# A hybrid decoder block: tile-wise pool waits, later value loads, products two groups behind their rows, and a gate tile taken into attention

## The chip, the cores and the metric

The kernel runs on one core of a Trainium2 chip. The metric is the device time of one execution in microseconds (us). The engines named below are TensorE (PE; its weight loads are PEld), VectorE (DVE), ScalarE (ACT), GpSimd (POOL) and SyncE (SP). Every DMA of this kernel is issued by SP, in one queue.

## The reference, cut to what matters

All is float32; S = D = 1024.

```python
h = rms_norm(x, g_pre)
qa, ka, va, fa, za, qb, kb, vb, zb, gates = split(h @ w_in)
# forgetting attention, 8 heads of 64: logits + c_t - c_s, c = cumsum(log_sigmoid(fa + b_forget))
ya = merge(softmax_causal(qa ka^T / 8 + c_t - c_s) va) * silu(za)
# differential attention, 4 heads: two softmaxes of 64-wide rotated q, k; values 128 wide
yb = (softmax_causal(q1 k1^T / 8) - lam * softmax_causal(q2 k2^T / 8)) vb
yb = merge(rms_norm(yb, g_subln) * (1 - lam_init)) * silu(zb)
gate_a, gate_b = split(sigmoid(gates))
merged = gate_a * (ya @ w_branch[0]) + gate_b * (yb @ w_branch[1])
x = x + rms_norm(merged @ w_out, g_post)
```

## The kernel before, in words

Float32 products are made from rounded high and low parts: a = hi + lo, and hi*hi + hi*lo + lo*hi are three matmuls. Five stages follow each other.

1. Value stage (0 to 111 us). x is normed and transposed to hT (1024 x 1024, in 128 x 512 blocks, high and low), and the values va, vb are projected and spilled to DRAM (va_d, vb_d).
2. Attention (111 to 604 us): units u = 0 to 3 are differential heads, u = 4 to 7 are pairs of forgetting heads. A unit's q and k are projected in 128 x 512 chunks (`project`, L246, 24 matmuls into pq or pk). For differential units `rope` copies the chunk out of PSUM (L283, ScalarE), swaps its halves by four DMAs of 64 KB (L287: swk, swq) and combines both (L288 to L290, VectorE and GpSimd). `stack` (L295 to L298) makes the high and low operands TA, TB, KA, KB; `swapped` (L407) makes by two DMAs the operands X0 and X1 with the partition halves exchanged. A group is two rows of queries: `s_row` multiplies (Sd or Sf, L421, L422), VectorE adds the bias and takes the maximum (L423), ScalarE the exponential (L428), GpSimd the scaling (L542). `av` transposes the rows on TensorE (ptd or ptf, L450), splits them into phf (L453, ScalarE) and plf (L454, VectorE), and multiplies by the values V (L474) into ypd or ypf, a PSUM pool (yps) with one buffer; `evac` empties it (L551 ScalarE, L552 VectorE) and stores it to y_d.
   Between the groups the list `fill` places other work: the next unit's projections, the z projections (pz, spilled to z_d), and the block sums t_d of hT.
3. Gate stage (604 to 750 us). The gate columns for output columns d = 0 (two tiles, one for each branch, of two chunks of 24 matmuls, `gates_plain`) are projected plainly; for d = 1 to 7 a Winograd scheme with seven half-size products is used (`wino`, L713), on the block sums loaded by `h_load` (T, eight loads of 1 MB, L795).
4. Branch stage (750 to 855 us, L846), 5. output stage (to the end).

The code is written in one order; a scheduler of the language then gives each engine its own order by its estimates of when inputs are ready. A pool hands out buffers by tag. Where a pool takes over memory that another pool has given back, its first users wait for the old pool's last users. Each engine runs its instructions in its order.

The lambda loads `lt` (L572) feed a few small VectorE instructions and one exponential (L575 to L581) ahead of the first unit.

The value loads come first in each unit:

```python
            def load():
                nc.sync.dma_start(f32(vt), src)
...
        pend = None
        for u in range(8):
            load, groups = unit_attn(u, T)
...
                for r in rws:
                    r()
                if pend:
                    pend()
                pend = prd
```

Of the kernel before, what the change touches and what calls it, by code (L numbers as in the profile page):

```python
# [16 lines left out]
P = 128  # L17
# [29 lines left out]
def tile_hybrid_block(  # L47
# [201 lines left out]


    with ExitStack() as st:
        qk = st.enter_context(tc.tile_pool(name="qk", bufs=2))
        pp = st.enter_context(tc.tile_pool(name="pp", bufs=6))
        ptp = st.enter_context(tc.tile_pool(name="ptp", bufs=3))
        stg = st.enter_context(tc.tile_pool(name="stg", bufs=2))
        pj = st.enter_context(tc.tile_pool(name="pj", bufs=2, space=PSUM))
        sps = st.enter_context(tc.tile_pool(name="sps", bufs=3, space=PSUM))
        tps = st.enter_context(tc.tile_pool(name="tps2", bufs=2, space=PSUM))
        yps = st.enter_context(tc.tile_pool(name="yps", bufs=1, space=PSUM))

        nc.sync.dma_start(gsub, g_subln.rearrange("o p -> p o"))
        nc.gpsimd.tensor_scalar(gsub, gsub, 1.0 - LAM_INIT, 1.0, op0=ALU.mult, op1=ALU.mult)
# [64 lines left out]
        def z_tasks(t):  # L327
            return spill_tasks(f"z{t}", (ZA + t * P) if t < 4 else (ZB + (t - 4) * P), z_d[t])

        def spill_tasks(nm, c0, dst):  # L330
            box = {}

            def mk(c):
                def run():
                    if not box:
                        box[0] = load_w(nm, w_cols(c0))
                    ps = pj.tile([P, CH], F32, tag="pj", name=f"p{nm}_{c}")
                    project(ps, box[0], c)
                    zs = stg.tile([P, CH], F32, tag="raw", name=f"s{nm}_{c}", bufs=3)
                    nc.scalar.copy(zs, ps)  # L340
                    nc.sync.dma_start(dst[:, c * CH:(c + 1) * CH], zs)
                return run
            return [mk(0), mk(1)]
# [57 lines left out]
        def swapped(T, m, g, nm):  # L401

            src = T["TB" if m else "TA"]
            qs = slice(2 * g * P, (2 * g + 2) * P)
            t = qk.tile([P, 2 * P], F32R, tag=f"X{m}", name=f"X{m}{nm}_{g}", bufs=3)
            for a, b in ((UPR, DNR), (DNR, UPR)):
                nc.sync.dma_start(f32(t[a]), f32(src[b, qs]))  # L407
            return t

        def s_row(T, m, i, X, bias, boff, nm):  # L410

# [73 lines left out]
        def unit_attn(u, T):  # L485

            diff = u < 4
            t = u if diff else u - 4
            vt = qk.tile([P, NB, 256], F32R, tag="V", name=f"V{u}")
            src = (vb_d if diff else va_d)[:, t, :].rearrange("(b p) c -> p b c", p=P)  # L490
            cb = []
            groups = []

            def load():
                nc.sync.dma_start(f32(vt), src)
                if not diff:
                    for m in range(2):
                        b = big.tile([P, S], F32, tag="big", name=f"cb{u}_{m}")
                        h = 2 * t + m
                        nc.sync.dma_start(b, cum_d[h:h + 1, :].to_broadcast([P, S]))  # L500
                        cb.append(b)

            if diff:
                def row(i, rows):
                    boff = S - (i + 1) * P
                    if "X" not in rows:
                        rows["X"] = [swapped(T, m, i // 2, f"d{u}") for m in range(2)]
                    p1, l1 = s_row(T, 0, i, rows["X"][0], dmask, boff, f"d{u}")
                    p2, l2 = s_row(T, 1, i, rows["X"][1], dmask, boff, f"d{u}")
                    n = (i + 1) * P  # L510
                    nc.vector.tensor_tensor(l2, l2, nlam, op=ALU.mult)  # L511
                    nc.gpsimd.tensor_scalar(  # L512
                        p2[:, 0:n], p2[:, 0:n], l2, 1.0, op0=ALU.mult, op1=ALU.mult)
                    nc.scalar.activation(p1[:, 0:n], p1[:, 0:n], AF.Copy, scale=l1)
                    nc.gpsimd.tensor_tensor(
                        p1[:, 0:n], p1[:, 0:n], p2[:, 0:n], op=ALU.add)
                    rows[i] = p1

                def evac(g):
                    def run(yp):  # L520
                        ys = stg.tile([P, 2 * P], F32, tag="ys", name=f"ys{u}_{g}")
                        nc.scalar.copy(ys, yp)
                        nc.sync.dma_start(y_d[u][:, g * 2 * P:(g + 1) * 2 * P], ys)
                    return run

                for g in GORD[u]:
                    rows = {}
                    groups.append((
                        4 * g + 3,
                        [lambda i=i, rows=rows: row(i, rows) for i in (2 * g, 2 * g + 1)],  # L530
                        lambda g=g, rows=rows: av(rows, g, vt, 0, False, evac(g), f"d{u}_{g}", False)))
            else:
                ysb = {}

                def row(m, i, rows):
                    n = (i + 1) * P
                    diag = cb[m][:, n - P:n]
                    nc.gpsimd.tensor_tensor(diag, diag, trim, op=ALU.add)  # L538
                    if "X" not in rows:
                        rows["X"] = swapped(T, m, i // 2, f"f{u}")  # L540
                    p1, l1 = s_row(T, m, i, rows["X"], cb[m], 0, f"f{u}")
                    nc.gpsimd.tensor_scalar(  # L542
                        p1[:, 0:n], p1[:, 0:n], l1, 1.0, op0=ALU.mult, op1=ALU.mult)
                    rows[i] = p1

                def evac(m, g):
                    def run(yp):
                        if m == 0:
                            ysb[g] = stg.tile([P, 2 * P], F32, tag="ys", name=f"ys{u}_{g}")
                        tmp = stg.tile([P, 2 * P], F32, tag="yt", name=f"yt{u}_{m}_{g}", bufs=1)  # L550
                        nc.scalar.copy(tmp[64:128], yp[64:128])  # L551
                        nc.vector.tensor_tensor(  # L552
                            ysb[g][64 * m:64 * m + 64], yp[0:64], tmp[64:128], op=ALU.add)
                        if m == 1:
                            nc.sync.dma_start(y_d[u][:, g * 2 * P:(g + 1) * 2 * P], ysb[g])
                    return run

                for g in GORD[u]:
                    for m in range(2):
                        rows = {}  # L560
                        groups.append((
                            4 * g + 3,
                            [lambda m=m, i=i, rows=rows: row(m, i, rows) for i in (2 * g + 1, 2 * g)],
                            lambda m=m, g=g, rows=rows: av(
                                rows, g, vt, m * P, True, evac(m, g), f"f{u}_{m}_{g}",
                                u == 7 and g in FING)))
            return load, groups


        lt = pp.tile([P, 4, 64], F32, tag="P", name="lt")  # L570
# [43 lines left out]
        T, tasks = unit_proj(0)  # L614
        for tk in tasks:
            tk()
        pend = None
        for u in range(8):
            load, groups = unit_attn(u, T)
            if u == 1:  # L620
                forget_sums()
            load()
# [10 lines left out]
            total = sum(s[0] for s in groups)  # L633
            done, nf = 0, 0
            for n, (wgt, rws, prd) in enumerate(groups):
                for r in rws:
                    r()
                if pend:
                    pend()
                pend = prd  # L640
                done += wgt
                while nf < len(fill) and nf < len(fill) * done / total:
                    fill[nf]()
                    nf += 1
        pend()

    bigs.close()

# [3 lines left out]


    gw = ExitStack()
    wx = gw.enter_context(tc.tile_pool(name="wx", bufs=2))
    tmp = gw.enter_context(tc.tile_pool(name="tmp", bufs=8))
    ydp = gw.enter_context(tc.tile_pool(name="ydp", bufs=1))
    xst = ExitStack()
    xps = xst.enter_context(tc.tile_pool(name="xps", bufs=8, space=PSUM))

    def split(dst, src, eng=nc.vector):

# [82 lines left out]


    tst = ExitStack()
    tpool = tst.enter_context(tc.tile_pool(name="tpool", bufs=1))

    yz = {}  # L750

# [24 lines left out]
        nc.sync.dma_start(g_d[d][br][:, c * CH:(c + 1) * CH], g)  # L776

    def gates_plain(d):
        for br in range(2):
            wt = load_w(f"g{br}_{d}", w_cols(GT + br * D + d * P), True, True)  # L780
            for c in range(2):
                ps = xps.tile([P, CH], F32, tag="x", name=f"pg{d}_{br}_{c}")
# [5 lines left out]
             for m, (kh, sh) in hB.items()}  # L788

    def h_load():  # L790
        for m in (4, 6, 5, 7):
            ts = [tpool.tile([P, 4, CH], F32R, tag=f"T{m}{part}", name=f"T{m}{part}")
                  for part in range(2)]
            for part in range(2):
                nc.sync.dma_start(f32(ts[part]), t_d[m][part])  # L795
            h_ops[m] = [[t[:, k, :] for k in range(4)] for t in ts]

    def gates_pair(d, order):
        raw = []
# [19 lines left out]
    tst.close()  # L819


    mpool = gw.enter_context(tc.tile_pool(name="mpool", bufs=1))
    mg = mpool.tile([P, KT, S], F32, name="mg")
    hslot = {(kh, sh): [(hpool, f"h{part}{kh}{sh}") for part in range(2)]
             for kh in range(2) for sh in range(2)}
# [202 lines left out]
```

## Time and profile before

| | |
|---|---|
| median of 3 runs | 946.88 us (944.96 to 947.32) |
| the profiled execution | 945.37 us |
| its span in the profile | 943.3 us |
| mean granted TensorE clock | 0.988 of full speed |
| busy: PE, DVE, ACT, POOL | 895.5, 625.4, 435.8, 489.3 us |
| DMA over the span | 136.95 MB, mean 145 GB/s |

A time in a profile row is from the start of the span. A row of the order of time has start, duration, engine, line, operation, output<-inputs, shapes and count, and in brackets how long the engine stood idle before it and which instruction ended that wait. A matmul of 512 columns that follows another starts 0.23 us after it, though its row says 0.39, since matmuls overlap.

### The profile page before, as it was taken

Reading aid. Unit: us, or ns where it says so; the run is one execution under the profiler, and the core shown is the slowest. Engines: PE = TensorE matmul, PEld = TensorE weight load, DVE = VectorE, ACT = ScalarE, POOL = GpSimd, SP = SyncE. Lnnn points to the kernel's source line nnn. Section 1 sums busy time; section 2 is a strip of 40 time slices with the busy share of each in tenths; the row PEclk is TensorE's granted clock in tenths of the full one; section 3 lists DMA queues with packets and bytes.
Section 4 is the critical chain, followed back from the end, with each engine's and each line's share of the span. In section 5 each row is a group of like instructions: output and inputs, shape, how many; then the busy total and the mean of one; then the engine's idle time right before and its main releaser. Section 6 shows DMA issues by size and latency. Waiting matters only on the chain. (4 is left out here: it accounts for less than half of the span.)

```text
span 943.3 us, 13785 instructions
## 1 busy us (share of the span) xinstructions
PE 895.5 (95%) x4600; PEld 750.5 (80%) x4600; DVE 625.4 (66%) x1180; ACT 435.8 (46%) x862; POOL 489.3 (52%) x461
## 2 busy tenths in 40 slices
PE   7999989999999999999999998899999999999993
PEld 5899868787887888888878887788888888887872
DVE  6731248988767778577767558515868893559766
ACT  3421115575656766465755648524443450324331
POOL 7200024446546448364554566407667436878963
PEclk9999999999999999999999999999999999999997
DMA  9532354424316163444542442496556596211332
GB/s 312 186 129 90 118 151 121 110 74 120 108 42 196 43 181 126 123 125 138 167 151 74 135 151 92 152 404 234 174 176 196 165 351 222 72 40 46 105 118 89
DMA packets 118664, 136.95 MB, mean 145 GB/s; under 512 B 10545, under 2 KB 84273, under 8 KB 117570
## 3 DMA queue, kind: packets, MB, share of 16 engines
q1 hardware_dynamic: 118594, 136.08, 45.6%
q8 instruction: 36, 0.59, 0.3%
q14 instruction: 34, 0.28, 0.1%
HBM read 85.65 MB, written 37.81 MB: 131 GB/s over the span
## 5 line engine op out<-in xcount | busy, mean ns | idle before, releaser
L195 PE MATMUL pv<-wvhi,hT 128*128 128x264 f32 (+2 forms) x384 | 89.6, 326 | 0.4 <-DVE hT L181 0.4
L246 PE MATMUL pk<-hT,hi_k 128*128 128x512 f32 x256 | 84.8, 404 | 4.0 <-DVE KB L298 2.2
L246 PE MATMUL pz<-hT,hi_z 128*128 128x512 f32 x256 | 84.3, 396 | 0.0
L246 PE MATMUL pq<-hT,hi_q 128*128 128x512 f32 x256 | 82.8, 397 | 0.0
L713 PE MATMUL x_o<-wo_op,a_o 128*128 128x512 f32 x336 | 77.9, 391 | 3.6 <-POOL a_o L665 2.3
L846 PE MATMUL pb<-yT,hi_br 128*128 128x512 f32 x256 | 78.5, 389 | 0.0
L713 PEld LDWEIGHTS x_o<-wo_op,a_o 128*128 128x128 f32 x336 | 62.7, 188 | 18.7 <-POOL a_o L665 3.7
L713 PE MATMUL x_g<-T,a_g 128*128 128x512 f32 x336 | 77.5, 389 | 0.0
L713 PEld LDWEIGHTS x_g<-T,a_g 128*128 128x128 f32 x336 | 63.1, 188 | 13.1
L195 PEld LDWEIGHTS pv<-wvhi,hT 128*128 128x128 f32 x384 | 64.7, 191 | 6.3 <-DVE hT L181 0.7
L542 POOL TENSOR_SCALAR Pf<-Pf,lf 128x1024 f32<-128x1024 f32 (+3 forms) x64 | 52.5, 822 | 30.6 <-DVE lf L430 27.5
L428 ACT ACTIVATE Pf<-Pf,mxf 128x1024 f32<-128x1024 f32 (+3 forms) x64 | 49.7, 777 | 31.3 <-DVE mxf L423 28.8
L428 ACT ACTIVATE Pd<-Pd,mxd 128x128 f32<-128x128 f32 (+7 forms) x64 | 49.5, 774 | 30.8 <-DVE mxd L423 29.1
L538 POOL TENSOR_TENSOR cb<-cb,trim 128x128 f32<-128x128 f32 x64 | 30.2, 474 | 61.8 <-DVE mxf L423 44.2
L195 PE MATMUL pv<-wvlo,hT 128*128 128x512 f32 (+2 forms) x192 | 61.9, 325 | 0.0
L512 POOL TENSOR_SCALAR Pd<-Pd,ld 128x128 f32<-128x128 f32 (+7 forms) x32 | 25.5, 798 | 69.7 <-DVE ld L511 37.8
L246 PEld LDWEIGHTS pk<-hT,hi_k 128*128 128x128 f32 x256 | 48.3, 193 | 14.5 <-DVE KB L298 2.4
L713 PE MATMUL x_g<-hT,a_g 128*128 128x512 f32 x252 | 58.6, 389 | 0.0
L454 DVE TENSOR_TENSOR plf<-ptf,phf 128x512 fp32r<-128x512 f32 (+1 forms) x80 | 49.6, 633 | 10.4 <-ACT phf L453 9.8
L846 PEld LDWEIGHTS pb<-yT,hi_br 128*128 128x128 f32 x256 | 48.1, 188 | 10.0
L713 PEld LDWEIGHTS x_g<-hT,a_g 128*128 128x128 f32 x252 | 47.3, 188 | 9.8
L246 PEld LDWEIGHTS pq<-hT,hi_q 128*128 128x128 f32 x256 | 47.5, 189 | 8.9
(248 smaller groups left out, 2424.4 us busy)
## 6 DMA issues: line engine op xcount, KB each, us to landing
t_d<-t SPq DMA_DIRECT2D x32, 256.0 KB, 2.2
T<-t_d SPq DMA_DIRECT2D x8, 1024.0 KB, 14.9
raw<-in_w_in_dram SPq DMA_DIRECT2D x14, 512.0 KB, 4.1
vb_d<-vbs SPq DMA_DIRECT2D x8, 512.0 KB
va_d<-vas SPq DMA_DIRECT2D x8, 512.0 KB, 3.7
raw_k<-in_w_in_dram SPq DMA_DIRECT2D x8, 512.0 KB, 5.3
raw_q<-in_w_in_dram SPq DMA_DIRECT2D x8, 512.0 KB
V<-vb_d SPq DMA_DIRECT2D x4, 1024.0 KB
```

The source lines that it names most:

```text
L195: nc.tensor.matmul(ps[n], lhsT=hT[hp][k // 4][i // 4][:, k % 4, hs], rhs=wt[k][:, a:b], start=first, stop=(k == KT - 1 and hp == 1))
L246: nc.tensor.matmul(ps, lhsT=a[:, k, :], rhs=hT[h][k // 4][c][:, k % 4, :], start=(k == 0 and a is hi and h == 0), stop=(k == KT - 1 and a ...
L428: nc.scalar.activation(pr[:, 0:n], pr[:, 0:n], AF.Exp, bias=mx[:, len(pcs) - 1:len(pcs)], scale=-1.0, accum_out=le)
L454: nc.vector.tensor_tensor(pl[:, 0:n], pt[:, 0:n], ph[:, 0:n], op=ALU.subtract)
L512: nc.gpsimd.tensor_scalar(p2[:, 0:n], p2[:, 0:n], l2, 1.0, op0=ALU.mult, op1=ALU.mult)
L538: nc.gpsimd.tensor_tensor(diag, diag, trim, op=ALU.add)
L542: nc.gpsimd.tensor_scalar(p1[:, 0:n], p1[:, 0:n], l1, 1.0, op0=ALU.mult, op1=ALU.mult)
L713: nc.tensor.matmul(x[m], lhsT=a[:, ai, k, :], rhs=right[m][bi][k], start=(k == 0 and n == 0), stop=(k == 3 and n == 2))
L846: nc.tensor.matmul(ps, lhsT=a[:, kk, :], rhs=yT[g][h][:, k % 2, sl], start=(k == 0 and a is hi and h == 0), stop=(k == 3 and a is lo))
```

## The change

- Most pools of attention and of the stages behind it get `reuse_waits="tile"`: a tile in reused memory waits only for the tiles that lay in its own bytes, not for the whole old pool. Some pools are put on the right side of memory.
- The value load V is taken out of `load` into `load_v`. It is put in a list and issued in `swapped`, right behind the X0 swap of the group that comes next; for units 1 to 7 from the middle of the unit before on.
- Forgetting units run their products two groups behind the rows instead of one (`pend` is a list).
- The first plain gate tile (branch 0, d = 0) leaves `gates_plain` and is written as two tasks between the last two products of attention, with its sigmoid (`gate_spill`) in attention's ScalarE order.
- The eight T tiles are created before their loads are issued.

```diff
-        qk = st.enter_context(tc.tile_pool(name="qk", bufs=2))
-        pp = st.enter_context(tc.tile_pool(name="pp", bufs=6))
+        qk = st.enter_context(tc.tile_pool(name="qk", bufs=2, reuse_waits="tile"))
+        pp = st.enter_context(tc.tile_pool(name="pp", bufs=6, side="right", reuse_waits="tile"))
...
+        def gate_spill(c, ps, zs):
+            nc.scalar.activation(zs, ps, AF.Sigmoid)
+            nc.sync.dma_start(g_d[0][0][:, c * CH:(c + 1) * CH], zs)
+
-        def spill_tasks(nm, c0, dst):
+        def spill_tasks(nm, c0, dst, out=None):
...
+                    if out:
+                        out(c, ps, zs)
+                        return
                     nc.scalar.copy(zs, ps)
...
             for a, b in ((UPR, DNR), (DNR, UPR)):
-                nc.sync.dma_start(f32(t[a]), f32(src[b, qs]))
+                lastx[0] = nc.sync.dma_start(f32(t[a]), f32(src[b, qs])).ins
+            if vload:
+                with tc.issue_after(lastx[0]):
+                    vload.pop(0)()
             return t
+
+        lastx, vload = [None], []
...
+            def load_v():
+                nc.sync.dma_start(f32(vt), src)
+
             def load():
-                nc.sync.dma_start(f32(vt), src)
...
-        pend = None
+        pend = []
+        nxt = None
         for u in range(8):
-            load, groups = unit_attn(u, T)
+            load, load_v, groups = nxt or unit_attn(u, T)
+            nxt = None
+            if u == 0:
+                vload.append(load_v)
...
             for n, (wgt, rws, prd) in enumerate(groups):
+                if n == len(groups) // 2 and u < 7:
+                    nxt = unit_attn(u + 1, T)
+                    vload.append(nxt[1])
                 for r in rws:
                     r()
-                if pend:
-                    pend()
-                pend = prd
+                pend.append(prd)
+                while len(pend) > (1 if u < 4 else 2):
+                    pend.pop(0)()
...
-        pend()
+        for tk, prd in zip(spill_tasks("g0_0", GT, None, gate_spill), pend):
+            tk()
+            prd()
...
     def gates_plain(d):
-        for br in range(2):
+        for br in range(1, 2):
...
     def h_load():
+
+        ts = {m: [tpool.tile([P, 4, CH], F32R, tag=f"T{m}{part}", name=f"T{m}{part}")
+                  for part in range(2)] for m in (6, 4, 7, 5)}
         for m in (4, 6, 5, 7):
-            ts = [tpool.tile([P, 4, CH], F32R, tag=f"T{m}{part}", name=f"T{m}{part}")
-                  for part in range(2)]
```

What this makes of the order on the engines, at three places. First SP at the start of attention, before (raw_k and raw_q are weights, va_d a store of values, V the values of units 0 and 1):

```order
L228 DMA raw_k_1401<-in_w_in_dram 128x8x128
L572 DMA lt<-in_lambda_q_dram 128x64
L572 DMA lt<-in_lambda_k_dram 128x64
L211 DMA va_d<-vas_1116 128x1024
L572 DMA lt<-in_lambda_q_dram 128x64
L572 DMA lt<-in_lambda_k_dram 128x64
L495 DMA V_1345<-vb_d 128x8x256
L495 DMA V_1912<-vb_d 128x8x256
L228 DMA raw_q_1514<-in_w_in_dram 128x8x128
L287 DMA swk_0_1210<-rawk_0_1208 32x512 x4
```

And after, at the same place:

```order
L228 DMA raw_k_1401<-in_w_in_dram 128x8x128
L211 DMA va_d<-vas_1116 128x1024
L228 DMA raw_q_1514<-in_w_in_dram 128x8x128
L287 DMA swk_0_1210<-rawk_0_1208 32x512 x4
L287 DMA swq_0_1255<-rawq_0_1253 32x512 x4
L287 DMA swk_1_1294<-rawk_1_1292 32x512 x4
L414 DMA X0d_0_1350<-TA_1173 64x256 x2
L507 DMA V_1345<-vb_d 128x8x256
L414 DMA X1d_0_1354<-TB_1174 64x256 x2
```

The lambda loads stand earlier now (among the stores of the value stage), the first value load behind the first X0 swap, the second seven rows further down.

Second TensorE in unit 7 near the end of attention, before (Sf are rows of scores):

```order
L421 MATMUL Sf_1_7_1_6298<-KB_5391,TB_5389 128x512
L422 MATMUL Sf_1_7_1_6298<-KB_5391,X1f_3_6289 128x512
L421 MATMUL Sf_1_6_0_6309<-KB_5391,TB_5389 128x512
L422 MATMUL Sf_1_6_0_6309<-KB_5391,X1f_3_6289 128x512
L421 MATMUL Sf_1_6_1_6313<-KB_5391,TB_5389 128x384
L422 MATMUL Sf_1_6_1_6313<-KB_5391,X1f_3_6289 128x384
```

And after (pg is the gate tile, its weights are hi_g and lo_g):

```order
L246 MATMUL pg_0_0_6849<-hT_92,hi_g_0_6845 128x512
L246 MATMUL pg_0_0_6849<-hT_88,lo_g_0_6846 128x512
L246 MATMUL pg_0_0_6849<-hT_88,hi_g_0_6845 128x512
L246 MATMUL pg_0_0_6849<-hT_92,hi_g_0_6845 128x512
L246 MATMUL pg_0_0_6849<-hT_88,lo_g_0_6846 128x512
L433 MATMUL Sf_1_6_0_6292<-KB_5374,TB_5372 128x512
L434 MATMUL Sf_1_6_0_6292<-KB_5374,X1f_3_6272 128x512
L246 MATMUL pg_0_0_6849<-hT_88,hi_g_0_6845 128x512
L246 MATMUL pg_0_0_6849<-hT_92,hi_g_0_6845 128x512
L246 MATMUL pg_0_0_6849<-hT_88,lo_g_0_6846 128x512
```

The 48 gate matmuls are spread in this way over about 100 rows between the scores and the transposes of the groups that were at 566 to 578 us; the rows behind them, the last products among them, stand as before.

Third ScalarE at the same place, after (sg is the gate tile's sigmoid, yt the evacuation of yps, Pf the exponentials):

```order
L440 ACTIVATE Pf_1_5_6450,lf_1_5_6460<-Pf_1_5_6450,mxf_1_5_6451 128x768
L687 CAST a_g_7057<-raw_0_7053 128x512
L331 ACT_TABLE_LOAD
L331 ACTIVATE sg_0_1_6919<-pg_0_1_6894 128x512
L687 CAST a_g_7075<-raw_0_7053 128x512
L465 CAST phf_0_3_3_6427<-ptf_0_3_3_6426 128x384
L465 CAST phf_1_3_0_6481<-ptf_1_3_0_6480 128x512
L440 ACT_TABLE_LOAD
L440 ACTIVATE Pf_1_4_6465,lf_1_4_6475<-Pf_1_4_6465,mxf_1_4_6466 128x640
L565 COPY yt_0_3_6443<-ypf_0_3_6390 64x256
```

Before, these rows of ScalarE held only casts, exponentials and evacuations; now a sigmoid with a table load on either side stands among them, and another such pair a few rows earlier.

More of the change, by code (lines that the diff above doesn't have):

```diff
@@ L251, in tile_hybrid_block @@
     with ExitStack() as st:
-        qk = st.enter_context(tc.tile_pool(name="qk", bufs=2))
-        pp = st.enter_context(tc.tile_pool(name="pp", bufs=6))
[L254 to L259, printed above, removed]
+        qk = st.enter_context(tc.tile_pool(name="qk", bufs=2, reuse_waits="tile"))
+        pp = st.enter_context(tc.tile_pool(name="pp", bufs=6, side="right", reuse_waits="tile"))
+        ptp = st.enter_context(tc.tile_pool(name="ptp", bufs=3, side="right", reuse_waits="tile"))
+        stg = st.enter_context(tc.tile_pool(name="stg", bufs=2, side="right", reuse_waits="tile"))
+        pj = st.enter_context(tc.tile_pool(name="pj", bufs=2, space=PSUM, reuse_waits="tile"))
+        sps = st.enter_context(tc.tile_pool(name="sps", bufs=3, space=PSUM, reuse_waits="tile"))
+        tps = st.enter_context(tc.tile_pool(name="tps2", bufs=2, space=PSUM, reuse_waits="tile"))
+        yps = st.enter_context(tc.tile_pool(name="yps", bufs=1, space=PSUM, reuse_waits="tile"))
         nc.sync.dma_start(gsub, g_subln.rearrange("o p -> p o"))
@@ L566, in unit_attn @@
                                 u == 7 and g in FING)))
-            return load, groups
+            return load, load_v, groups
         lt = pp.tile([P, 4, 64], F32, tag="P", name="lt")
@@ L644, in tile_hybrid_block @@
                     nf += 1
-        pend()
+        for tk, prd in zip(spill_tasks("g0_0", GT, None, gate_spill), pend):
+            tk()
+            prd()
     bigs.close()
     gw = ExitStack()
-    wx = gw.enter_context(tc.tile_pool(name="wx", bufs=2))
-    tmp = gw.enter_context(tc.tile_pool(name="tmp", bufs=8))
-    ydp = gw.enter_context(tc.tile_pool(name="ydp", bufs=1))
+    wx = gw.enter_context(tc.tile_pool(name="wx", bufs=2, side="right", reuse_waits="tile"))
+    tmp = gw.enter_context(tc.tile_pool(name="tmp", bufs=8, side="right", reuse_waits="tile"))
+    ydp = gw.enter_context(tc.tile_pool(name="ydp", bufs=1, side="right", reuse_waits="tile"))
     xst = ExitStack()
-    xps = xst.enter_context(tc.tile_pool(name="xps", bufs=8, space=PSUM))
+    xps = xst.enter_context(tc.tile_pool(name="xps", bufs=8, space=PSUM, reuse_waits="tile"))
     def split(dst, src, eng=nc.vector):
@@ L747, in tile_hybrid_block @@
     tst = ExitStack()
-    tpool = tst.enter_context(tc.tile_pool(name="tpool", bufs=1))
+    tpool = tst.enter_context(tc.tile_pool(name="tpool", bufs=1, reuse_waits="tile"))
     yz = {}
@@ L790, in h_load @@
     def h_load():
+        ts = {m: [tpool.tile([P, 4, CH], F32R, tag=f"T{m}{part}", name=f"T{m}{part}")
+                  for part in range(2)] for m in (6, 4, 7, 5)}
         for m in (4, 6, 5, 7):
-            ts = [tpool.tile([P, 4, CH], F32R, tag=f"T{m}{part}", name=f"T{m}{part}")
-                  for part in range(2)]
             for part in range(2):
-                nc.sync.dma_start(f32(ts[part]), t_d[m][part])
-            h_ops[m] = [[t[:, k, :] for k in range(4)] for t in ts]
+                nc.sync.dma_start(f32(ts[m][part]), t_d[m][part])
+            h_ops[m] = [[t[:, k, :] for k in range(4)] for t in ts[m]]
     def gates_pair(d, order):
@@ L819, in tile_hybrid_block @@
     tst.close()
-    mpool = gw.enter_context(tc.tile_pool(name="mpool", bufs=1))
+    mpool = gw.enter_context(tc.tile_pool(name="mpool", bufs=1, reuse_waits="tile"))
     mg = mpool.tile([P, KT, S], F32, name="mg")
```

## The prediction

> **What bounds the kernel now.** I read the page first, then the busy time by stretches, then the waits and the order of time on each engine inside the stretches where TensorE is not busy.
>
> ```profile
> PE 895.5 (95%) x4600; PEld 750.5 (80%) x4600; DVE 625.4 (66%) x1180; ACT 435.8 (46%) x862; POOL 489.3 (52%) x461
> ```
>
> TensorE is the bound. Its work is the same before and after (the same matmuls, in another order), so the change can gain only where TensorE stands still or runs slowly. The stretches show where that is:
>
> ```profile
> 132.00:144.00 12.00, 8.19 (x30) 6.12 (x29) 11.67 (x11) 4.49 (x8) 5.51 (x5) 0.86 0.22 55
> ...
> 161.00:178.00 17.00, 14.80 (x71) 11.96 (x71) 15.83 (x32) 9.94 (x20) 9.29 (x8) 0.90 0.37 92
> 178.00:564.00 386.00, 376.50 (x2067) 318.99 (x2066) 280.21 (x682) 230.47 (x478) 206.88 (x213) 1.00 0.41 122
> ...
> 604.00:750.00 146.00, 146.00 (x644) 120.91 (x645) 87.72 (x98) 55.80 (x98) 81.80 (x57) 1.00 0.69 232
> ...
> 566.00:578.00 12.00, 9.75 (x60) 7.52 (x58) 11.15 (x37) 10.40 (x20) 8.88 (x10) 1.00 0.52 165
> 578.00:604.00 26.00, 22.09 (x157) 18.58 (x156) 20.71 (x62) 19.94 (x49) 12.66 (x23) 1.00 0.06 22
> ```
>
> The columns are length, then busy time of PE, PEld, DVE, ACT, POOL, the granted clock, the DMA share and GB/s. The start of attention (132 to 178 us) and its end (566 to 604 us) lose time; the gate stage (604 to 750 us) loses none, so each matmul taken out of it makes it shorter by that matmul's time. The middle of attention loses 9.5 of 386 us in small pieces.
>
> **Term A, the start: transfers in another order.** The change moves the lambda loads forward among the value stage's stores, and puts the first value load V0 behind the first X0 swap and the second, V1, behind a later one. Before, both value loads (1 MB each) stood ahead of the weights of q and of the rotary swap swk:
>
> ```profile
> 114.67 1.41 SPq L495 DMA_DIRECT2D V<-vb_d  x2
> 117.87 2.37 SPq L228 DMA_DIRECT2D raw_q<-in_w_in_dram  x1
> 120.33 4.68 SPq L287 DMA_DIRECT2D swk<-rawk  x4
> ...
> 135.72 2.41 SPq L287 DMA_DIRECT2D swk<-rawk  x4
> ...
> 140.52 1.19 SPq L407 DMA_DIRECT2D X1d<-TB  x2
> ```
>
> ```profile
> swk<-rawk SPq DMA_DIRECT2D x4, 64.0 KB, 6.5
> ```
>
> ```profile
> swk<-rawk SPq DMA_DIRECT2D x32, 64.0 KB, 2.0
> ```
>
> The first of the last two lines is of 112 to 131 us alone: issue to landing took 6.5 us there, against 2.0 over the whole kernel; and four issues took 4.68 us, against 2.41 later. What waited for it:
>
> ```profile
> 130.20 1.80 POOL L289 TENSOR_TENSOR swk<-swk,sinT 128x512 f32<-128x512 f32 x1 [19.21 <-DMA swk<-rawk]
> ```
>
> ```profile
> 130.16 0.69 DVE L288 TENSOR_TENSOR rawk<-rawk,cosT 128x512 f32<-128x512 f32 x1 [8.77 <-DMA swk<-rawk]
> ...
> 137.32 1.22 DVE L236 TENSOR_TENSOR lo_k<-raw_k,hi_k 128x1024 fp32r<-128x1024 f32 x1
> ```
>
> ```profile
> 133.83 0.62 ACT L295 CAST KA<-rawk 64x512 fp32r<-64x512 f32 x1 [10.01 <-DVE rawk L290]
> 134.47 0.61 ACT L297 CAST KB<-rawk 64x512 fp32r<-64x512 f32 x1
> 135.11 0.59 ACT L283 COPY rawk<-pk 128x512 f32<-128x512 f32 x1
> ```
>
> ```profile
> 117.89 0.50 PE L246 MATMUL pq<-hT,lo_q 128*128 128x512 f32 x1 [0.62 <-DVE lo_q L236]
> ...
> 135.84 0.70 PE L246 MATMUL pk<-hT,hi_k 128*128 128x512 f32 x2 [1.76 <-ACT rawk L283]
> 138.59 0.51 PE L246 MATMUL pk<-hT,lo_k 128*128 128x512 f32 x1 [2.04 <-DVE lo_k L236]
> ...
> 145.25 0.22 PE L422 MATMUL Sd<-KB,X1d 128*128 128x128 f32 x1
> ```
>
> The copy at 135.11 only empties a PSUM buffer, but ScalarE works in order and stands behind the casts of KA and KB, which wait for the swap. The lo_k at 137.32 stands behind the same swap on VectorE. After: swk can issue when raw_q has, some 0.5 us behind 117.87 (a later issue of one such load takes about that), takes 2.4 us for four and lands 2 us on, so at 122.8 instead of 130.16: 7.4 us earlier. TensorE wants the PSUM buffer at 134.08 (135.84 less its wait) and gets it at about 128.3; it wants lo_k 2.04 us before 138.59 and gets it about 5 us before that. Both waits go: 3.8 us, the idle time of that stretch (12 less 8.19). The granted clock of 0.86 over 12 us is another 1.7 us lost, and it follows these waits (in 161 to 178 us 0.90 over 17 us, again 1.7, behind one wait of 1.91 us). I count it as going with them. The 0.62 us at 117.89 goes too: lo_q stood behind lambda's VectorE work, which waited for its load. Sum 6.1.
>
> The page "TensorE: Matmul & The Clock Gate" of the Trainium skill (Part 1, What's actually happening) says that the clock halves after an idle window of about 3.4 us. No single wait here is that long, and the rows show the low clock behind 1.9 us, so the trace decides; by that rule the 1.7 us would not hang on these waits, and A would be smaller by it.
>
> In 161 to 178 us TensorE loses 2.2 us of idle time and 1.7 us of clock, behind a VectorE that is busy for 15.83 of 17 us. VectorE starts 7.4 us earlier, TensorE 5.5 us: the 1.9 us between is what a wait there can shrink. I take 1.4 of the 3.9 us. Against it stands V0, now ahead of the X1 swap. That swap was issued at 140.52 to 141.71, lands 2 us on (143.1) and is used at 145.25: 2.1 us of slack. One megabyte at the 426 GB/s below is 2.5 us, and its issue 0.5: 0.9 us too late at worst. I take 0.5. **A = 6.1 + 1.4 - 0.5 = 7.0**, between 3.8 (the two waits alone) and 10.
>
> **Term B, the end: the gate tile.** The first gate tile's 48 matmuls leave the gate stage and stand among the rows and transposes of unit 7's first groups, in what was 566 to 578 us. They do not stand between the last products, whose order is that of before.
>
> ```profile
> 566.82 0.28 PE L474 MATMUL ypf<-phf,V 128*128 128x256 f32 x1
> 566.93 0.28 PE L474 MATMUL ypf<-plf,V 128*128 128x256 f32 x1
> ...
> 569.40 0.50 PE L421 MATMUL Sf<-KB,TB 128*128 128x512 f32 x1 [0.72 <-DVE mxf L423]
> ...
> 571.48 0.50 PE L421 MATMUL Sf<-KA,TA 128*128 128x512 f32 x1 [0.86 <-DVE mxf L423]
> ...
> 603.91 0.74 PE L246 MATMUL pg<-hT,hi_g 128*128 128x512 f32 x2 [0.91 <-DVE ys L552]
> ...
> 625.85 5.60 PE L713 MATMUL x_g<-hT,a_g 128*128 128x512 f32 x24
> 631.29 2.88 PE L713 MATMUL x_g<-T,a_g 128*128 128x512 f32 x12
> ```
>
> Two tiles took 603.91 to 625.85, so one is 10.97 us off the gate stage. What does it cost where it goes? The 60 matmuls of 566 to 578 us are mostly of 256 columns or between 128 and 512, and follow each other 0.117 us apart when nothing is waited for: 7.0 us of work in 12. So up to 5.0 us is free; the idle time by the rows is 2.25 us, the lower bound. Since 10.97 us of independent work is spread over every wait there, I take 4.9. The wait of 0.91 us at 603.91 goes as well (the gate's PSUM pool waited for attention's last evacuation; the second tile now waits tile by tile): 0.9.
>
> Against it, ScalarE. The gate tile's values pass through a sigmoid there, twice, between exponentials: four more table loads.
>
> ```profile
> 608.85 1.28 ACT L775 ACT_TABLE_LOAD   x1
> 610.15 0.60 ACT L775 ACTIVATE g<-pg 128x512 f32<-128x512 f32 x1
> ```
>
> The first two loads and one sigmoid fall in the stretch: 10.40 + 2.56 + 0.60 and one early cast of a_g at 0.6 is 14.2 us in a stretch of about 18 (12 + 10.97 - 4.9), so there is room. The other sigmoid is the trouble: it waits for the tile's last matmul, and behind it in ScalarE's order stand the cast of phf, which TensorE needs about 2 us later (12 products of 0.117 us and some transposes), and behind the fourth load the evacuation of yps, a pool of one buffer. Its own load runs ahead while it waits; sigmoid 0.6 and the load back 1.28 are on the path: 1.8 us; lo_g, now on VectorE (1.22 us like lo_k above), has the stretch's room. Bounds: 0 and two full loads with both sigmoids, 3.8. **B = 4.9 + 0.9 - 1.8 = 4.0**, between -0.6 and 5.8.
>
> The page "ScalarE: Activation LUTs" of the Trainium skill (What ACT_TABLE_LOAD costs) gives a switch 1.28 us and a drain of about 1.38 us besides. The rows put the next ACTIVATE 1.30 us behind the load's start, with no drain seen; by the page four switches would cost 5.5 us more of ScalarE, and B would be nearer 1.
>
> **Costed at nothing.** The products of units 4 to 7 two groups behind their rows: the order on TensorE had them that late already, apart from unit 7's first three groups, which the gate tile pushes back. Value loads of units 1 to 7 in mid-unit: covered unless they hold a swap up (below). The T loads:
>
> ```profile
> 608.80 5.68 SPq L795 DMA_DIRECT2D T<-t_d  x8
> ```
>
> ```profile
> 616.00:620.00 4.00, 4.00 (x20) 3.30 (x19) 0.29 (x1) 0.56 (x2) 1.29 (x1) 1.00 1.02 426
> ```
>
> Eight of 1 MB at 426 GB/s are 20 us. They now go first of all, three ahead of attention's last store, so about 6 us earlier against the end of attention, while their first use comes 10.97 us earlier: at 16.3 us behind that end (10.97 and 24 matmuls in 5.4). The four pairs land at some 5, 10, 15 and 20 us and are wanted at 16, 19, 22 and 24.5: nothing waits. Tile-wise pool waits elsewhere, and yd and yf behind T: used 40 us or more later. From the gate pairs on, TensorE's order is the same.
>
> **Sum.** 945.37 (the profiled execution, span 943.3) - 7.0 - 4.0 = 934.4. That execution lies 1.5 us under the median of the runs, 946.88, so the forecast is 935.5.
>
> **Rivals.** Changes within 0.3% (2.8 us) can't be told from none.
> 1. The fill buys nothing (B about 0): the stretch already has VectorE at 11.15 and ScalarE at 10.40 of 12 us, and the new work of ScalarE takes the gain back. 939.5; for it the rows of the second sigmoid, against it the room worked out above.
> 2. The fill pays fully: the tile's whole 10.97 us hide, because the last groups' softmax runs ahead during it and the waits of 578 to 604 us (3.9 us idle) shrink too. 945.4 - 7 - 10 + 1.5 = 930. Against it: the last groups' products keep their order and their one buffer.
> 3. The start's gain is given back in the next unit, or the reordered middle loses some 5 us more than the 9.5 it loses now: 941 to 946, around no change.
> 4. Slower: value loads ahead of X1 swaps. If in units 1 to 7 too the swap comes 0.9 us too late and each such wait brings the low clock (1.7), that is 2.6 us a unit, 18 for seven: 953. It takes the 11 us from five units on. Against it: before, the value loads of mid attention also stood between swaps, and no wait of TensorE for a swap is in the list of waits.
>
> **Chances.** Forecast (931 to 939) 0.53, rival 1 0.17, rival 2 0.13, rival 3 0.11, rival 4 0.06. Faster takes the forecast, 1, 2 and a third of 3; same most of the rest of 3. The range leaves out a part of rivals 2 and 3 and all of 4.
>
> **What would show it.** The swap lands near 123 us and no wait of over 1 us stands in 132 to 144 us, with the clock at 1.0 (A); the 48 gate matmuls lie ahead of the last four groups in a stretch of some 18 us, and a wait for phf or for yps of 1 to 2 us follows the second sigmoid (B); no wait for T in the gate stage. Wrong would be: waits for X swaps, a late T, or TensorE as idle in the longer stretch as it was.

## The result, and the profile after

| | before | after |
|---|---|---|
| median (range) of 4 runs | 947.1 us (944.96 to 948.29) | 937.46 us (936.66 to 939.99) |
| ratio to before, 95% interval | | 0.9905 (0.9879 to 0.9931) |
| the changed kernel timed again (below) | | 0.992 (0.9901 to 0.9939) |
| profiled execution, its span | 945.37, 943.3 us | 936.66, 934.7 us |

The forecast was 935.5 us, with a chance of 0.53 on 931 to 939. The kernel is some 9 us faster; 11 were forecast. The terms of the sum came out otherwise than worked out.

Where the gain arises is read from the start of the same instruction in both traces. The table gives by how many us the changed kernels stand ahead of the kernel before (943.3 us execution) at seven places; the kernels of the later rows are described below. TensorE has done the same matmuls ahead of each place in every kernel, but for the fourth q chunk: there the kernel before has done 20 matmuls of scores, e3_v_first 12 and the other changed kernels 18. By their columns (512 in 0.23 us) the others' gains there are too good by some 0.3 us, and that of e3_v_first by 1.7, an estimate.

| us ahead at: | first matmul of attention (111.18 before) | fourth q chunk (159.96) | last z chunk (558.06) | first Winograd product (625.85) | first branch product (759.13) | second branch chunk (765.21) | end |
|---|---|---|---|---|---|---|---|
| after | -0.8 | 6.0 | 9.3 | 10.5 | 10.0 | 8.9 | 8.6 |
| after, again | 0.7 | 7.4 | 13.3 | 12.8 | 12.3 | 11.3 | 11.0 |
| e1_no_gate | 0.0 | 6.7 | 10.9 | 7.6 | 7.2 | 7.5 | 7.6 |
| e2_late_sigmoid | 0.0 | 4.4 | 9.2 | 14.2 | 9.5 | 5.6 | 5.4 |
| e3_v_first | -0.4 | 4.6 | 4.3 | 4.3 | -1.5 | -4.0 | -4.4 |
| e4_one_behind | 0.5 | 4.6 | 9.2 | 10.1 | 9.5 | 9.0 | 9.3 |
| e5_v_order_alone | 0.1 | 3.6 | 5.2 | 3.5 | 3.5 | 3.2 | 3.2 |
| e6_yd_later | 0.2 | 6.8 | 9.8 | 14.7 | 12.4 | 11.1 | 11.4 |
| e7_branch_weights_first | -0.3 | 3.7 | 7.4 | 12.1 | 11.6 | 11.2 | 10.8 |

So in the profiled execution, which comes to attention 0.8 us late: 6.9 us in the start of attention, 3.3 us in its middle, 1.2 us at its end with the gate tile, and 1.9 us given back behind it.

The profile after: TensorE's busy time, then the stretches (same columns as before).

```profile
PE 893.5 (96%) x4600; PEld 752.6 (81%) x4600; DVE 629.0 (67%) x1181; ACT 441.5 (47%) x865; POOL 493.9 (53%) x461
```

```profile
132.00:144.00 12.00, 12.00 (x58) 10.03 (x57) 8.57 (x13) 3.63 (x8) 4.85 (x3) 1.00 0.61 163
...
161.00:178.00 17.00, 15.99 (x73) 12.88 (x73) 15.73 (x32) 8.41 (x16) 10.12 (x7) 0.90 0.55 139
```

TensorE no longer stands still in 132 to 144 us. The swap of the first chunk, on SP and at GpSimd:

```profile
117.07 0.38 SPq L228 DMA_DIRECT2D raw_q<-in_w_in_dram  x1
118.32 2.53 SPq L287 DMA_DIRECT2D swk<-rawk  x4
...
133.02 1.15 SPq L414 DMA_DIRECT2D X0d<-TA  x2
134.22 0.58 SPq L507 DMA_DIRECT2D V<-vb_d  x1
134.89 1.21 SPq L414 DMA_DIRECT2D X1d<-TB  x2
```

```profile
122.52 1.81 POOL L289 TENSOR_TENSOR swk<-swk,sinT 128x512 f32<-128x512 f32 x1 [10.76 <-DMA swk<-rawk]
```

It is there at 122.52 us instead of 130.20. The end of attention, in four stretches:

```profile
556.00:578.00 22.00, 22.00 (x129) 19.34 (x128) 14.18 (x45) 16.72 (x29) 12.05 (x15) 1.00 0.34 110
578.00:582.00 4.00, 2.98 (x17) 1.94 (x16) 2.47 (x5) 3.97 (x6) 2.05 (x3) 1.00 0.18 68
582.00:590.00 8.00, 6.45 (x40) 5.98 (x37) 4.69 (x13) 5.61 (x14) 2.70 (x5) 0.79 0.00 0
590.00:605.00 15.00, 12.72 (x90) 10.56 (x89) 11.50 (x35) 11.38 (x30) 7.40 (x13) 1.00 0.16 36
```

With the gate tile in it, 556 to 578 us has no idle time. Right behind it ScalarE is busy for 3.97 of 4 us, and TensorE waits, then runs at the low clock (0.79 over 8 us is 1.7 us). ScalarE and TensorE there:

```profile
577.68 1.28 ACT L331 ACT_TABLE_LOAD   x1
578.97 0.60 ACT L331 ACTIVATE sg<-pg 128x512 f32<-128x512 f32 x1
579.47 0.61 ACT L687 CAST a_g<-raw 128x512 fp32r<-128x512 f32 x1
579.98 0.97 ACT L465 CAST phf<-ptf 128x384 fp32r<-128x384 f32 x2
580.96 1.28 ACT L440 ACT_TABLE_LOAD   x1
582.26 0.83 ACT L440 ACTIVATE Pf<-Pf,mxf 128x640 f32<-128x640 f32 x1
582.99 0.19 ACT L440 ACTIVATION_READ_ACCUMULATOR Pf<-Pf,mxf 128x1 f32 x1
583.20 0.37 ACT L565 COPY yt<-ypf 64x256 f32<-64x256 f32 x1
```

```profile
579.35 0.50 PE L433 MATMUL Sf<-KB,TB 128*128 128x512 f32 x1 [0.39 <-DVE mxf L435]
580.51 0.38 PE L486 MATMUL ypf<-phf,V 128*128 128x256 f32 x1 [0.43 <-ACT phf L465]
581.10 0.38 PE L486 MATMUL ypf<-plf,V 128*128 128x256 f32 x1 [0.21 <-DVE plf L466]
...
584.07 0.39 PE L486 MATMUL ypf<-phf,V 128*128 128x256 f32 x1 [1.52 <-DVE ys L566]
```

TensorE's waits from 604 to 760 us, by who was waited for (total, times, longest): none is for T; the longest stands at the start of the branch stage.

```profile
PE pb L870 <- POOL lo_br L236: 0.9, 1, 0.9
```

### The profile page after: what moved, and what is told of

The parts are those of the page before. It is cut to its first block, busy times and chain, and to the rows that moved or that the text cites. A ratio compares the mean times of both kernels' runs of the same rounds, so it can differ in the third digit from the quotient of the medians.

```text
span 934.7 us, 13764 instructions
## 1 busy us (share of the span) xinstructions
PE 893.5 (96%) x4600; PEld 752.6 (81%) x4600; DVE 629.0 (67%) x1181; ACT 441.5 (47%) x865; POOL 493.9 (53%) x461
## 5 line engine op out<-in xcount | busy, mean ns | idle before, releaser
L246 PE MATMUL pk<-hT,hi_k 128*128 128x512 f32 x256 | 82.8, 399 | 2.0 <-DVE KB L298 2.0
L736 PEld LDWEIGHTS x_g<-T,a_g 128*128 128x128 f32 x336 | 63.1, 188 | 13.3
L246 PEld LDWEIGHTS pk<-hT,hi_k 128*128 128x128 f32 x256 | 48.0, 191 | 11.6 <-DVE KB L298 2.4
L736 PEld LDWEIGHTS x_g<-hT,a_g 128*128 128x128 f32 x252 | 47.3, 188 | 10.1
## 6 DMA issues: line engine op xcount, KB each, us to landing
T<-t_d SPq DMA_DIRECT2D x8, 1024.0 KB, 11.3
```

What stands on the lines that cost most here:

```text
L246: nc.tensor.matmul(ps, lhsT=a[:, k, :], rhs=hT[h][k // 4][c][:, k % 4, :], start=(k == 0 and a is hi and h == 0), stop=(k == KT - 1 and a ...
L736: nc.tensor.matmul(x[m], lhsT=a[:, ai, k, :], rhs=right[m][bi][k], start=(k == 0 and n == 0), stop=(k == 3 and n == 2))
```

## The experiments

All were timed against the kernel before: e1, e2, e3 and e5 on one chip (945.39 us there), e4, e6, e7 and the repeat on another (944.86 us). A low stretch is a time in which the trace's clock record shows half the full clock: one of 3.41 us costs 1.7 us, one of 6.83 us costs 3.4.

**The gate tile put back.**

```diff
-        for tk, prd in zip(spill_tasks("g0_0", GT, None, gate_spill), pend):
-            tk()
-            prd()
+        for prd in pend:
+            prd()
...
-        for br in range(1, 2):
+        for br in range(2):
```

> The changed kernel with the first gate tile put back into the gate stage, all else kept. Theory: the tile in attention is worth only the 1.3 us by which the two traces part between the last z projection (9.3 us ahead) and the second gate tile (10.6 us ahead), so this runs at about 938.8 us, and the first Winograd product starts about 9.3 us ahead of the kernel before. Rival, the prediction's term B: the tile is worth 4 us, and the run comes out at 941.5 us. A second rival: the tile costs as much as it brings, and the run stays at 937.5 us or below.

Measured: ratio 0.9944 (0.9927 to 0.9961), which is the rival's size: 0.9944 of 947.1 is 941.8 us. By the table it is 10.9 us ahead at the last z chunk and only 7.6 at the first Winograd product, so without the tile the end of attention costs 3.3 us more than before. Its longest wait there, and the stretch:

```profile
563.71 0.69 PE L433 MATMUL Sf<-KB,TB 128*128 128x384 f32 x1 [3.91 <-DVE mxf L435]
```

```profile
560.00:572.00 12.00, 8.25 (x42) 7.28 (x43) 10.36 (x27) 7.63 (x17) 7.03 (x9) 0.72 0.47 141
```

TensorE waits for VectorE's maxima, and 3.4 us go to the low clock behind the wait (0.72 over 12 us), which is the whole loss. In the wait VectorE itself stands still for a store of block sums, then takes 2.32 us for a row that took 0.69 at 557.72, while GpSimd works on lo_g (from 560.15 for 2.35 us):

```profile
560.73 2.32 DVE L378 TENSOR_TENSOR t<-f,t 128x512 fp32r<-128x512 f32 x1 [1.72 <-DMA t_d<-t]
```

In the second trace of the changed kernel the same row takes 2.92 us, at 555.98, and TensorE, with the tile's matmuls at hand, does not wait. Against e1 the tile is worth 4.5 us by the traces (1.2 and 3.3; 1.7 of it is that e1 has twice the low clock there) and 2.3 to 3.7 by the ratios, whose intervals overlap; against the end of attention before, 1.2.

**The sigmoids behind attention.** In attention the gate tile is copied; the sigmoids run behind the last evacuation.

```diff
-            nc.scalar.activation(zs, ps, AF.Sigmoid)
-            nc.sync.dma_start(g_d[0][0][:, c * CH:(c + 1) * CH], zs)
+            nc.scalar.copy(zs, ps)
+            raw_g.append((c, zs))
...
+        with tc.issue_after(lasty[0]):
+            for c, zs in raw_g:
+                nc.scalar.activation(zs, zs, AF.Sigmoid)
+                nc.sync.dma_start(g_d[0][0][:, c * CH:(c + 1) * CH], zs)
```

> The changed kernel, where the gate tile is only copied out of PSUM in attention, and its two sigmoids run behind the last evacuation of attention (four table loads become none there). Theory: the second sigmoid with its two table loads made the waits of 0.4, 0.4, 0.2 and 1.5 us at 579 to 584 us and the low clock behind them (1.7 us); most of this goes, so about 934 us, with no low clock between 578 and 605 us. Rival: the ScalarE row that waits for the last gate matmul is the cause, whatever it computes; then the waits stay and the run is at 936.5 to 937.5 us.

Measured: ratio 0.9936 (0.991 to 0.9963): the time forecast was missed. In attention the theory held: 9.2 us ahead at the last z chunk, 14.2 at the first Winograd product, so its end gains 5.0 us instead of 1.2, and the waits behind the tile and the low clock are gone:

```profile
556.00:578.00 22.00, 22.00 (x129) 19.34 (x128) 15.16 (x46) 14.94 (x29) 12.52 (x16) 1.00 0.31 98
578.00:600.00 22.00, 19.11 (x137) 16.16 (x135) 17.26 (x51) 16.60 (x42) 10.57 (x18) 1.00 0.04 13
```

But 8.6 us are given back behind attention. Waits of 4.4 us stand at two places, and from 749.63 to 759.62 us the clock is 0.66, another 3.4 us:

```profile
652.50 4.83 PE L742 MATMUL x_g<-hT,a_g 128*128 128x512 f32 x20 [1.17 <-DVE a_g L694]
```

```profile
749.63 1.22 PE L876 MATMUL pb<-yT,hi_br 128*128 128x512 f32 x4 [2.07 <-ACT hi_br L232]
751.11 0.79 PE L876 MATMUL pb<-yT,hi_br 128*128 128x512 f32 x2 [0.26 <-DVE cu_g L735]
752.75 0.79 PE L876 MATMUL pb<-yT,lo_br 128*128 128x512 f32 x1 [0.85 <-POOL lo_br L236]
```

with the DMA engines full up to the first, and ScalarE in order ahead of the second:

```profile
625.00:650.00 25.00, 25.00 (x110) 20.29 (x108) 12.85 (x18) 9.27 (x17) 11.06 (x8) 1.00 1.05 363
```

```profile
744.75 3.87 ACT L865 CAST yT<-yf 128x1024 fp32r<-128x1024 f32 x4
748.53 1.04 ACT L232 CAST hi_br<-raw_br 128x1024 fp32r<-128x1024 f32 x1
```

**The loads of yd (2 MB) behind the third pair's weights**, added to the last one.

```diff
-    for t in (4, 5, 6, 7, 0, 1, 2, 3):
+    for t in (4, 5, 6, 7):
...
+        if d == 3:
+            with tc.issue_after(lastraw[0]):
+                for t in range(4):
+                    y_load(t)
```

> The sigmoids behind attention as in the run before, and the four loads of yd (2 MB) issued behind the weights of the third pair instead of ahead of them. Theory: with the attention's end 4 us earlier, the gate stage is bound by the transfers of its first 50 us, and gives 1.8 us back at 652 us; with 2 MB less ahead of the weights that wait of 1.3 us goes, but the branch stage's start may still wait for its casts: ratio 0.989 to 0.992. Rival: the queue is not what was late; the wait at 652 us stays and the ratio is 0.9936 as before.

Measured: ratio 0.9895 (0.9873 to 0.9917). The wait at 652 us is gone (TensorE busy for 5.00 of 5 us, where the last kernel had 3.80):

```profile
650.00:655.00 5.00, 5.00 (x23) 4.12 (x23) 4.41 (x5) 3.88 (x7) 5.00 (x4) 1.00 0.93 288
```

So the transfers were late there. The wait for hi_br stayed, 1.68 us, and of 14.7 us 3.6 were lost by the second branch chunk. The ratio is where it was expected (0.989 to 0.992); the intervals of this and the last kernel still touch.

**The first branch weights cast ahead of yT**, added again.

```diff
+    wbr = load_br(0, 0)
     yT = {}
     for g, ss in ((2, eslot[0:2]), (3, eslot[2:4]), (0, hslot[0, 0]), (1, hslot[1, 0])):
```

> As the last one, and the first branch weights are cast on ScalarE ahead of the four casts of yT (3.9 us) instead of behind them. Theory: TensorE waited for hi_br 2.1 us, then for lo_br 0.9 us, with 3.4 us of low clock, because ScalarE runs in order; with the cast first these go and 3 to 5 us of the gain in attention are kept: ratio 0.985 to 0.988, the branch stage starting with no wait above 1 us. Rival: yT itself is late, and the wait only changes its name: ratio as of the last one.

Measured: ratio 0.9882 (0.9863 to 0.9901), 934.0 us, the fastest kernel here and just behind the 0.985 to 0.988 expected; the changed kernel on the same chip 0.992. The cast now stands first, and the branch stage starts with a wait of 0.3 us:

```profile
743.55 1.03 ACT L232 CAST hi_br<-raw_br 128x1024 fp32r<-128x1024 f32 x1
744.48 3.89 ACT L878 CAST yT<-yf 128x1024 fp32r<-128x1024 f32 x4
```

```profile
748.22 0.50 PE L889 MATMUL pb<-yT,hi_br 128*128 128x512 f32 x1 [0.30 <-DVE yT L879]
```

Of 12.1 us ahead 11.2 are kept at the second branch chunk: by the traces 2.7 us more than in the last kernel. The medians differ by 1.5 us only, and the intervals of the two ratios overlap; that the order of the cast is worth it in the runs is likely, not shown.

**Products one group behind again.**

```diff
-                while len(pend) > (1 if u < 4 else 2):
+                while len(pend) > 1:
...
-        for tk, prd in zip(spill_tasks("g0_0", GT, None, gate_spill), pend):
-            tk()
-            prd()
+        tk = spill_tasks("g0_0", GT, None, gate_spill)
+        tk[0]()
+        pend[0]()
+        tk[1]()
```

> The changed kernel with the products of forgetting units one group behind their rows again; the gate tile then stands around the last product alone. Theory: the order of units 4 to 6 was that late already, so it changes little: 0.988 to 0.995 of the kernel before, and the last z projection starts 8.5 to 10 us ahead of it. Rival: two groups behind is what let the gate tile fill the waits; then the stretch of the gate tile grows, the second tile starts at least 2 us later than the changed kernel's, and the ratio is above 0.995.

Measured: ratio 0.9931 (0.9912 to 0.9949), 9.2 us ahead at the last z chunk. The theory held: two groups against one change nothing that the runs tell from the changed kernel's 0.992. The end of attention gains 0.9 us here, with one long wait behind the tile instead of several:

```profile
584.26 1.11 PE L462 MATMUL ptf<-ident,Pf 128*128 128x128 f32 x4 [3.97 <-DVE plf L466]
```

**Value loads first again, tile-wise waits kept.**

```diff
             def load():
+                nc.sync.dma_start(f32(vt), src)
                 if not diff:
...
-            if u == 0:
-                vload.append(load_v)
...
-                if n == len(groups) // 2 and u < 7:
-                    nxt = unit_attn(u + 1, T)
-                    vload.append(nxt[1])
```

> The changed kernel with the value loads at the start of each unit again; tile-wise waits and the gate tile kept. Theory: the two value loads ahead of the rotary swap made the swap late; here they come about 5 us before it, so half of the delay returns: 940 to 943 us, with a first swap landing later than 123 us and waits of TensorE of over 1 us in 130 to 144 us. Rival: the lambda loads and pool-wise waits held the queue, and with tile-wise waits the value loads are out of the way in time: 937 to 938.5 us, no such wait.

Measured: ratio 1.0041 (1.0026 to 1.0055), slower than both theories gave, and for another reason. The start has no long wait (0.67 us the longest in 110 to 144 us): with tile-wise waits both value loads are issued before attention and the swap is early.

```profile
110.34 1.00 SPq L510 DMA_DIRECT2D V<-vb_d  x2
...
117.91 2.53 SPq L287 DMA_DIRECT2D swk<-rawk  x4
```

```profile
123.29 1.54 POOL L289 TENSOR_TENSOR swk<-swk,sinT 128x512 f32<-128x512 f32 x1 [11.96 <-DMA swk<-rawk]
```

The rival was right there. The loss lies ahead of 558 us (4.3 us ahead there, against 9.3; with the missing scores counted, 2.8 of these 5 us stand at the fourth q chunk already, the rest in the middle), where the scheduler made another order, and behind attention, where it goes from 4.3 us ahead to 4.0 behind, mostly at the branch stage's start:

```profile
760.65 2.93 PE L866 MATMUL pb<-yT,hi_br 128*128 128x512 f32 x6 [3.02 <-ACT hi_br L232]
```

What in that order costs the 5 us was not tried.

**The order of the value loads alone, in the kernel before.**

```diff
-                nc.sync.dma_start(f32(t[a]), f32(src[b, qs]))
+                lastx[0] = nc.sync.dma_start(f32(t[a]), f32(src[b, qs])).ins
+            if vload:
+                with tc.issue_after(lastx[0]):
+                    vload.pop(0)()
```

> The kernel before with the value loads moved behind the X swaps and nothing else: pool-wise waits, lambda loads at the old place, products one group behind, gate tile in the gate stage. Theory: this move alone carries the start's gain, so 940 to 941 us, the two waits of 1.8 and 2.0 us at 135 to 139 us and the low clock gone, the wait of 0.6 us at 118 us kept. Rival: the tile-wise waits are needed for it, and this runs at 945 us or above.

Measured: ratio 0.9939 (0.9919 to 0.9958), 939.5 us. The theory held: the two long waits are gone, the small one stays, and the swap is there at 123.40:

```profile
117.75 0.50 PE L246 MATMUL pq<-hT,lo_q 128*128 128x512 f32 x1 [0.60 <-DVE lo_q L236]
```

```profile
123.40 1.71 POOL L289 TENSOR_TENSOR swk<-swk,sinT 128x512 f32<-128x512 f32 x1 [12.51 <-DMA swk<-rawk]
```

Either the order (here) or the tile-wise waits (the kernel ahead of this one) is enough to bring the swap forward. Like the kernel without the tile, this one loses at the end of attention (5.2 us ahead, then 3.5); a low stretch at 568 us, 1.7 us, is as much as the loss.

**The changed kernel again.**

> The changed kernel once more, unaltered, on the chip of these runs. Expected from the first comparison: ratio 0.9905 of the kernel before (0.988 to 0.993), the stretch of the gate tile without a wait, then waits of 0.4 to 1.7 us and a low clock behind the second sigmoid, and 1 us of wait at the start of the branch stage.

Measured: ratio 0.992 (0.9901 to 0.9939), as expected. In its trace the end of attention brings nothing (13.3 us ahead, then 12.8): its first wait behind the tile is 1.71 us, for a maximum that stands on VectorE behind the low part of a_g (an operand of the first Winograd products, cast early), and the low clock lasted twice as long, 0.57 over 8 us:

```profile
577.00:585.00 8.00, 7.01 (x28) 5.88 (x29) 3.90 (x10) 5.76 (x11) 2.48 (x3) 0.57 0.10 35
```

## Why the prediction was right in the sum, and where its steps failed

- **The sum.** The terms give 934.4 us in the profiled execution and, with the 1.5 us between it and the median, 935.9; the forecast says 935.5. That the measured median lies within 2 us of it is in part luck: the start and the middle gained more than their parts (6.9 and 3.3 us in the profiled execution, against 5.6 and 1.4), which made up for some of what the end and the stage behind it lacked (1.2 and -1.9, against 4.0 and 0).
- **The start, 7.0 us: its main parts right.** The swap was expected at 122.8 us and is used at 122.52; both waits and the low clock behind them are gone. From the first matmul of attention to the fourth q chunk 6.9 us are gained (6.8 in the second trace), for which the parts of 6.1 and -0.5 stand. TensorE's idle time falls from 4.4 to 0.2 us and the clock rises from 0.97 to 1.00 (first row before, second after):

```profile
111.18:159.96 48.78, 44.35 (x194) 35.82 (x193) 28.87 (x54) 15.58 (x35) 14.45 (x13) 0.97 0.53 142
112.03:153.94 41.91, 41.69 (x192) 34.36 (x190) 24.78 (x45) 14.16 (x32) 13.51 (x11) 1.00 0.54 147
```

  The 0.5 us for V0 ahead of the X1 swap did not come in the two traces of the changed kernel. It did in e2, e4, e5 and e7, which issue V between the same swaps: there TensorE waits 0.7 to 0.9 us for X1 (the row is e4's), and the same gain is 3.4 to 4.4 us. So whether it falls due differs from execution to execution, and the exact figure owes something to luck.

```profile
PE Sd L434 <- DMA X1d<-TB: 0.9, 1, 0.9
```

  The part for the next unit, 1.4 us, lies behind that place: in 161 to 178 us the idle time falls from 2.2 to 1.0 us, which is near it, and the clock stays at 0.90.
- **The middle, costed at nothing but for that part: mis-sized.** It brought 3.3 us (5.9 in the second trace). With the value loads behind the swaps it gains 1.6 to 5.9 us; with them first it stays about even by the table (4.6 us ahead, then 4.3), and gains some 1.4 us if the missing scores are counted. Part of the spread is the clock: between the two places the kernel before has two low stretches, the changed kernel three, e5 two, e3, e4 and e6 one, and the second trace, e1, e2 and e7 none. Against a kernel without any, 3.4 us of the gain are the clock's; in the changed kernel's first trace the clock costs 1.7 instead. Which instruction brings the rest was not separated.
- **The fill, 4.9 + 0.9 us: near.** The stretch of the tile has no idle time, and with the sigmoids out of the way the end gains 5.0, 4.9 and 4.7 us in three kernels.
- **The second sigmoid, -1.8 us: the term that failed.** Measured against those three the sigmoids cost 3.7 us in the profiled execution (1.2 us left of 4.9) and over 5 in the second trace. In the first trace the place was the one named: the casts of phf, then the evacuation of yps behind the load back. What was left out is the low clock that follows such waits, 1.7 us and 3.4 us, though the same price had been counted at the start; without it some 2.0 us remain in either trace, near the 1.8. The three kernels move both sigmoids, so the cost is that of both; how it divides was not tried. The trace shows no drain behind a table load: loads at 577.68 and 580.96, the next ACTIVATE 1.29 and 1.30 us later, so the trace does not agree with the drain on the page "ScalarE: Activation LUTs" of the Trainium skill (What ACT_TABLE_LOAD costs). By the prediction's estimate from that page B would have been near 1, close to the 1.2 measured, but not for its reason.
- **Behind attention, nothing: failed.** T came in time, as worked out. But 1.7 us are lost between the first Winograd product and the second branch chunk, and up to 8.6 us where the end of attention was faster. A stage that TensorE fills was taken to shrink by what is taken out; its transfers and the casts at its end were not sized against the shorter cover.
- **Rival 1** (the fill buys nothing) came nearest at the end of attention, **rival 3**'s giving back came in another stage; **rival 4** did not come: a wait for a swap shows at most once in a trace.

## What to carry to other kernels

Independent matmuls do fill another stage's waits, but what follows them should not go on an engine that works in order and empties a single buffer there: a copy in place and the function later was worth about 4 us at the end of attention here, by the traces, and the median came below the changed kernel's only when the transfers and casts behind were moved too. A stage that one engine fills to the brim hides a second bound: before it is made shorter, add up its transfers and the last casts ahead of the next stage. And a head start of the bounding engine can be lost at the next stretch where it waits for another engine; filler that stands ready there can keep it, as the tile did against e1.

## What was unexpected of the hardware

The low clock follows some waits of about 2 us and not others. The same wait, for KB, in the changed kernel and in the fastest one, with the ten us around it:

```profile
481.61 0.73 PE L246 MATMUL pk<-hT,hi_k 128*128 128x512 f32 x2 [2.00 <-DVE KB L298]
```

```profile
478.00:488.00 10.00, 8.00 (x33) 6.18 (x31) 5.27 (x15) 3.75 (x10) 2.67 (x7) 0.83 0.61 194
```

```profile
485.06 0.74 PE L246 MATMUL pk<-hT,hi_k 128*128 128x512 f32 x2 [1.98 <-DVE KB L298]
```

```profile
482.00:492.00 10.00, 8.02 (x44) 6.57 (x43) 5.76 (x14) 4.08 (x12) 2.28 (x6) 1.00 0.58 184
```

One loses another 1.7 us to the clock (0.83 over 10), the other none. This fits the free-running window that the page "TensorE: Matmul & The Clock Gate" of the Trainium skill describes (Part 1, What's actually happening), though not its idle time of about 3.4 us: 2.0 us are enough here, and 1.44 at 161.85 us of the changed kernel.

The clock records of the ten traces bear the window out. Within a trace the changes of the clock lie a multiple of 3.413 us apart. On that grid the first wait (479.61 to 481.61) lies in one window, 479.49 to 482.91, and the low stretch is the next window; the second is split at 484.55 into 1.47 and 0.51 us. In each window at full clock that a low one follows, TensorE is idle for 1.44 us or more. But some windows with up to 1.87 us are not followed by one, so between these two figures something else decides, and that stays open.

So some us of difference between two executions of one kernel are the window's: in its first 900 us the changed kernel has four low stretches of 3.41 us in the first trace, 6.8 us lost, and one of 6.83 us in the second, 3.4 lost.
